# Two of the three split products of a 256-token segment taken as one 512-column stream

## The chip, the core and the metric

The kernel runs on one core of one Trainium2 chip. The metric is device microseconds of one execution. Before the change the median of three runs is 1772.79 us, from 1772.46 to 1773.16 us. The profile comes from one further execution, which took 1773.86 us, with 1771.5 us from its first to its last instruction. Its mean granted TensorE clock is 0.989 of full speed.

## The reference, cut to what matters

Two layers work on 768 tokens: 512 latent tokens and 256 context tokens, each 1024 wide. A layer mixes the tokens (four attention-like groups), projects the result back with the output weights, adds it to the stream, and then applies a gated feed-forward network (FFN) with a width-3 convolution over tokens. The second layer returns only the latent tokens.

```python
D_MODEL, SEQ, CTX_LEN, D_FF, DEPTH = 1024, 512, 256, 2816, 2

def dwconv3(x, w):
    xp = jnp.pad(x, ((0, 0), (1, 1), (0, 0)))
    return xp[:, :-2] * w[0] + xp[:, 1:-1] * w[1] + xp[:, 2:] * w[2]

# per layer, latent and context alike:
#   x = x + gate1 * (heads @ w_out)                      output projection
#   h = modulate(rmsnorm(x), shift, scale)
#   up = dwconv3(h @ w_up, w_conv) + b;  g, v = split(up)  up projection, 2 x 2816 wide
#   x = x + gate2 * ((silu(g) * v) @ w_down)             down projection
```

(The last four lines give the reference's loop body in short; the first part is word for word, apart from the constants being on one line.)

## The kernel before

Activations stand transposed: channels on the 128 partitions, tokens along the free dimension, so the 1024 channels are 8 tiles (`KT`). Each fp32 matrix product is made of three fp32r products: a weight is split into a rounded part `wh` and a rest `wl` (line 474 on ScalarE, line 478 on VectorE or GpSimd), an activation into `yh` and `yl`, and `product` (line 488) issues for each k-tile wh·yh, wh·yl and wl·yh into one PSUM tile. `self.mm` (line 73) records every matmul, so that all matmuls carry that line.

**Segments.** In layer 0 the tokens run as a 512-token segment and a 256-token context segment (`SEGS`). In layer 1 only 512 tokens are left; the output projection and the last part of the down projection run them as two halves of 256 (`HALVES`), the rest as one segment of 512. So 256-column matmuls stand at five places: the output projection of layer 0 for context (8 output tiles x 8 k-tiles = 64 k-steps), the up projection of layer 0 for context (44 units x 8 = 352), the down projection of layer 0 for context (8 x 22 = 176), the output projection of layer 1 (2 halves x 64 = 128), and the last chunk of the down projection of layer 1 (2 x 8 x 7 = 112). Together 832 k-steps.

**Output projection** (`w_out`): for each output tile eight k-steps into a PSUM bank `po`, then `residual` (line 883, VectorE): x = x + gate · po. While it runs, `tick` weaves in steps of the norm of the segment that is already done (`yt`, `yh`, `yl`, lines 397 to 407), in the order in which the program issues them on VectorE.

**FFN** (`ffn`): it is done in three chunks of 8, 7 and 7 pairs (`CHUNKS`). A pair is a gate unit and a value unit. A unit (`up`) takes eight k-steps into a PSUM tile `pu` of 1024 columns, of which there are two: latent in columns 0 to 511, context in 512 to 767. Then ScalarE writes `up` from `pu` (line 910), and VectorE adds the two outer taps of the convolution, reading `pu` (lines 912 and 915, each once for latent and once for context). `pu` is free after the last of these. The gate unit gets silu on ScalarE (line 926); the value unit is multiplied on GpSimd (line 935), rounded on ScalarE (`g`, line 937) and its rest formed on GpSimd (line 938). After each value unit of layer 0 up to two jobs from `todo` run: each is a pair of scans (`junk`, line 305, VectorE) that makes modulation numbers for later. After a chunk the down projection of its pairs runs into banks `pd`, each followed by `residual`.

The order on each engine is that in which the Python code issues the work; every engine takes its instructions in that order.

Of the kernel before, what the change touches and what calls it, by code (L numbers as in the profile page):

```python
# [16 lines left out]
KT = 8  # L17
SEQ = 512
# [34 lines left out]
class Trunk:  # L53
# [34 lines left out]
    def build(self):  # L88
# [1 line left out]
        ctx = self.ctx  # L90
        self.const = ctx.enter_context(self.pool("const", 1))
        self.wp = ctx.enter_context(self.pool("wp", 1))
        self.s3 = ctx.enter_context(self.pool("s3", 16))
        self.os = ctx.enter_context(self.pool("os", 3))
        self.sm = ctx.enter_context(self.pool("sm", 1))
        self.ps = ctx.enter_context(self.pool("ps", 1, space=bass.MemoryType.PSUM))
# [73 lines left out]
        for l in range(DEPTH):  # L170
# [29 lines left out]
                    self.tick(1)  # L200
            first = [self.up_open(l, 0, gv, True) for gv in range(2)]
            a, b = segs[0]
            part = lambda u, k0, k1: lambda: self.product(u[1][:, a:b], u[0], y, a, b, range(k0, k1))
            self.woven(steps, part(first[0], 0, 4), part(first[0], 4, 8), part(first[1], 0, 8))
            a, b = segs[1]
            self.pin = ALL
# [36 lines left out]
        fes.close()  # L243

    def new_y(self):
        return [tuple(self.s3.tile([128, T], F32R, tag="s3", name=n) for n in ("yh", "yl")) for _ in range(KT)]

    def mixing_pools(self, es):
        mk = lambda n, b: es.enter_context(self.pool(n, b, reuse_waits="tile"))
# [139 lines left out]
    def norm_apply(self, x, y, sg, A, sh, r, ks):  # L389
        nc = self.nc  # L390
        a, b = sg
        n = b - a
        j = 0 if b <= SEQ else 1
        for k in ks:
            t = self.u.tile([128, T], F32, tag="u", name="yt")
            yh, yl = y[k]
            i = nc.vector.scalar_tensor_tensor(out=t[:, :n], in0=x[k][:, a:b], scalar=A[:, k, j:j + 1],
                                               in1=r[:, :n], op0=ALU.mult, op1=ALU.mult)
            if self.ticking:
                self.tc.keep_in_program_order(i)  # L400
            nc.scalar.activation(out=yh[:, a:b], in_=t[:, :n], func=AF.Identity, bias=sh[:, k, j:j + 1])
            if self.slow and k % 2:
                nc.gpsimd.tensor_tensor(out=t[:, :n], in0=t[:, :n],
                                        in1=sh[:, k, j:j + 1].broadcast_to([128, n]), op=ALU.add)
                nc.gpsimd.tensor_tensor(out=yl[:, a:b], in0=t[:, :n], in1=f32v(yh[:, a:b]), op=ALU.subtract)  # L405
            else:
                nc.vector.scalar_tensor_tensor(out=yl[:, a:b], in0=t[:, :n], scalar=sh[:, k, j:j + 1],  # L407
                                               in1=f32v(yh[:, a:b]), op0=ALU.add, op1=ALU.subtract)
# [79 lines left out]
    def product(self, ps, w, y, a, b, ks=None):  # L488
        wh, wl = w
        n = len(y)  # L490
        for k in ks or range(n):
            yh, yl = y[k]
            self.mm(ps, lhsT=wh[:, k, :], rhs=yh[:, a:b], start=(k == 0), stop=False)
            self.mm(ps, lhsT=wh[:, k, :], rhs=yl[:, a:b], start=False, stop=False)
            self.mm(ps, lhsT=wl[:, k, :], rhs=yh[:, a:b], start=False, stop=(k == n - 1))


    def early_start(self, l, fast=False):
# [369 lines left out]
    def load_o(self, NT):  # L868
        nc = self.nc
        s = []  # L870
        for k in range(KT):
            g = self.g.tile([128, 2, T], F32R, tag="g", name="og")
            if k in self.kept:
                o = self.kept[k]
                nc.scalar.copy(out=g[:, 0, :NT], in_=o[:, :NT])
                nc.vector.tensor_tensor(out=g[:, 1, :NT], in0=o[:, :NT], in1=f32v(g[:, 0, :NT]), op=ALU.subtract)
            else:
                nc.sync.dma_start(out=f32v(g[:, :, :NT]), in_=self.od[:, k, :, :NT])
            s.append((g[:, 0], g[:, 1]))
        return s  # L880

    def residual(self, p, x, gate, m, a, b):
        self.nc.vector.scalar_tensor_tensor(out=x[m][:, a:b], in0=p[:, :b - a],  # L883
                                            scalar=gate[:, m, (0 if b <= SEQ else 1):(1 if b <= SEQ else 2)],
                                            in1=x[m][:, a:b], op0=ALU.mult, op1=ALU.add)

    def w_out(self, l, s, x, sg):
        a, b = sg
        for m in range(KT):
            w = self.weights(("wout", l, m), b - a == 256, m % 3 == 2 and l == 0)  # L890
            p = self.bank("tp", "po")
            self.product(p[:, :b - a], w, s, a, b)
            self.residual(p, x, self.mod[l][:, 16:24], m, a, b)
            self.tick(2 if m < 3 else 1)
        self.tick(KT)
# [2 lines left out]
    def up_open(self, l, i, gv, fast=False):  # L898
        return self.weights(("wup", l, i, gv), fast), self.ps.tile([128, 1024], F32, tag="sc", bufs=2, name="pu")

    def up(self, l, i, gv, y, segs, NT, opened=None):
        nc = self.nc
        w, p = opened or self.up_open(l, i, gv)
        if not opened:
            for a, b in segs:
                self.product(p[:, a:b], w, y, a, b)
        c0 = O_CONV + 4 * (i + NF * gv)
        cw = self.par[l][:, c0:c0 + 4]
        u = self.u.tile([128, T], F32, tag="u", name="up")
# [9 lines left out]
    def ffn(self, l, x, y, segs, first, todo, after):  # L919
# [10 lines left out]
        for k0, k1 in CHUNKS:  # L930
            G = []
            for i in range(k0, k1):
# [3 lines left out]
                gt = self.g.tile([128, 2, T], F32R, tag="g", name="g")  # L936
                nc.scalar.copy(out=gt[:, 0, :NT], in_=uv[:, :NT])
                eng.tensor_tensor(out=gt[:, 1, :NT], in0=uv[:, :NT], in1=f32v(gt[:, 0, :NT]), op=ALU.subtract)  # L938
                G.append((gt[:, 0], gt[:, 1]))
                for _ in range(2):  # L940
                    if todo:
                        todo.pop(0)()
# [3 lines left out]
            for sweep in sweeps:  # L946
                for m in range(KT):
                    w = self.weights(("wdn", l, m, k0, k1), sweep[0][1] - sweep[0][0] == 256,
                                     k1 == NF and m % 3 == 2 and l == 1)
                    for a, b in sweep:  # L950
                        p = self.bank("tp", "pd")
                        self.product(p[:, :b - a], w, G, a, b)
# [446 lines left out]
```

## Time and profile before

| | before |
|---|---|
| median of three runs | 1772.79 us |
| the profiled execution | 1773.86 us |
| its span | 1771.5 us |
| PE busy | 1676.8 us (95%) |
| DVE busy | 997.5 us (56%) |
| ACT busy | 788.7 us (45%) |
| POOL busy | 892.3 us (50%) |

PE is TensorE's matmul side, DVE is VectorE, ACT is ScalarE, POOL is GpSimd. Busy time is a mean over stages: an engine at 56% overall can be the one that everything waits for in one stage. A matmul's duration in the trace covers its way through the array; the next one starts before it ends, so the cost of one in a stream is the distance from one start to the next.

### The profile page before, as it was taken

What the parts mean: (1) busy time and instruction counts of PE and PEld (TensorE: products, weight loads), DVE (VectorE), ACT (ScalarE), POOL (GpSimd) and SP (SyncE); (2) the same over time, 40 slices, a digit from 0 to 9 for tenths busy, and PEclk for the clock granted to TensorE, in tenths of its full rate; (3) what the DMA queues carried; (4) which work ended last, traced back from release to release, by engine and by line L of the source; (5) the groups of instructions that cost most, each with busy time, mean ns of one, the idle gap of its engine ahead of it and who ended that gap; (6) DMA issues with size and microseconds to landing.
All of it is one profiled execution on the core that took longest, in us unless ns stands there. A gap on an engine that the chain in (4) does not pass through costs nothing. (4 is left out here: it accounts for less than half of the span.)

```text
span 1771.5 us, 26688 instructions
## 1 busy us (share of the span) xinstructions
PE 1676.8 (95%) x10212; PEld 1444.5 (82%) x10212; DVE 997.5 (56%) x1739; ACT 788.7 (45%) x1355; POOL 892.3 (50%) x700
## 2 busy tenths in 40 slices
PE   6899999899999999999999988999999999999997
PEld 4678778798888888888888786887789888888887
DVE  3577768653677854844255476886765522122245
ACT  4276655553543321332133354775654543242343
POOL 1323124665665643654365665323775666565663
PEclk9999999899999999999999999999999999999999
DMA  8665535336433332334343545542447333333334
GB/s 332 180 204 195 155 108 185 93 113 238 150 101 128 110 119 95 129 114 118 106 131 119 176 146 170 155 124 85 143 120 238 111 96 95 96 96 96 105 104 135
DMA packets 78447, 244.16 MB, mean 138 GB/s; under 512 B 9072, under 2 KB 12656, under 8 KB 78192
## 3 DMA queue, kind: packets, MB, share of 16 engines
q1 hardware_dynamic: 78320, 242.46, 43.5%
q8 instruction: 81, 1.33, 0.3%
q14 instruction: 46, 0.38, 0.1%
HBM read 214.64 MB, written 27.79 MB: 137 GB/s over the span
## 5 line engine op out<-in xcount | busy, mean ns | idle before, releaser
L478 POOL TENSOR_TENSOR wl<-raw,wh 128x1024 fp32r<-128x1024 f32 (+3 forms) x228 | 501.2, 2200 | 630.5 <-ACT wh L474 606.7
L474 ACT CAST wh<-raw 128x1024 fp32r<-128x1024 f32 (+1 forms) x228 | 233.6, 1027 | 356.0 <-PE pd L73 185.6
L73 PE MATMUL pu<-yh,wh 128*128 128x512 f32 (+1 forms) x1072 | 377.9, 353 | 6.0 <-DVE up L915 5.8
L73 PE MATMUL pu<-yl,wh 128*128 128x512 f32 (+1 forms) x1072 | 377.2, 352 | 1.5 <-POOL yl L405 1.3
L73 PE MATMUL pu<-yh,wl 128*128 128x512 f32 (+1 forms) x1072 | 376.4, 351 | 0.0
L73 PE MATMUL pd<-g,wh 128*128 128x512 f32 (+1 forms) x1168 | 289.3, 339 | 5.7 <-DVE x L883 3.7
L912 DVE SCALAR_TENSOR_TENSOR up<-pu,par,up 128x511 f32<-128x511 f32 (+1 forms) x132 | 83.1, 657 | 292.7 <-ACT up L910 291.2
L73 PEld LDWEIGHTS pu<-yh,wh 128*128 128x128 f32 x1072 | 202.8, 189 | 35.3 <-issue 6.2
L73 PEld LDWEIGHTS pd<-g,wh 128*128 128x128 f32 x1168 | 201.7, 191 | 31.6 <-ACT wh L474 3.9
L73 PEld LDWEIGHTS pu<-yl,wh 128*128 128x128 f32 x1072 | 202.8, 189 | 29.4 <-POOL yl L405 1.9
L73 PEld LDWEIGHTS pu<-yh,wl 128*128 128x128 f32 x1072 | 202.6, 189 | 27.1
L73 PE MATMUL pj<-yh,wh 128*128 128x512 f32 (+1 forms) x608 | 216.9, 360 | 6.9 <-ACT ev L552 4.4
L73 PE MATMUL pj<-yl,wh 128*128 128x512 f32 (+1 forms) x608 | 213.1, 351 | 1.6 <-DVE yl L407 1.4
L73 PE MATMUL pj<-yh,wl 128*128 128x512 f32 (+1 forms) x608 | 212.6, 350 | 0.1
L73 PE MATMUL pd<-g,wl 128*128 128x512 f32 (+1 forms) x584 | 197.3, 339 | 4.1 <-DVE wl L478 3.5
L305 DVE SCALAR_TENSOR_TENSOR junk<-mrow,cbc 128x1024 f32<-128x1024 f32 x80 | 155.3, 1942 | 1.5 <-DMA mrow<-in_wmodt 0.6
L883 DVE SCALAR_TENSOR_TENSOR x<-pd,mod,x 128x512 f32<-128x512 f32 (+1 forms) x80 | 48.8, 614 | 173.2 <-PE pd L73 173.0
L73 PEld LDWEIGHTS pj<-yh,wh 128*128 128x128 f32 x608 | 116.6, 192 | 26.2 <-ACT ev L552 7.3
L73 PEld LDWEIGHTS pj<-yh,wl 128*128 128x128 f32 x608 | 117.0, 192 | 15.1 <-POOL wl L478 0.5
L647 POOL TENSOR_TENSOR p<-p,rec 128x512 f32<-128x512 f32 (+2 forms) x80 | 79.7, 998 | 97.5 <-DVE rec L643 87.0
L73 PEld LDWEIGHTS pj<-yl,wh 128*128 128x128 f32 x608 | 117.4, 193 | 13.0 <-DVE yl L407 2.7
L73 PEld LDWEIGHTS pd<-g,wl 128*128 128x128 f32 x584 | 111.4, 191 | 17.0 <-DVE wl L478 4.3
(174 smaller groups left out, 2729.7 us busy)
## 6 DMA issues: line engine op xcount, KB each, us to landing
raw<-in_wup SPq DMA_DIRECT2D x88, 512.0 KB, 3.5
mrow<-in_wmodt SPq DMA_DIRECT2D x56, 512.0 KB, 3.6
raw<-in_win SPq DMA_DIRECT2D x44, 512.0 KB, 3.7
raw<-in_wdn SPq DMA_DIRECT2D x48, 448.0 KB, 3.4
mraw<-in_wmod SPq DMA_DIRECT2D x40, 512.0 KB, 7.3
raw<-in_wout SPq DMA_DIRECT2D x32, 512.0 KB, 3.5
qk<-hl SPq DMA_DIRECT2D x16, 768.0 KB, 3.5
stk<-qk SPq DMA_DIRECT2D x32, 384.0 KB, 5.6
```

What stands on the lines that cost most here:

```text
L73: i = self.nc.tensor.matmul(out, **kw)
L305: self.tc.keep_in_program_order(nc.vector.scalar_tensor_tensor(out=junk, in0=raw, scalar=1.0, in1=self.cbc[:, i], op0=ALU.mult, op1=ALU.mu ...
L474: i = nc.scalar.copy(out=wh, in_=raw)
L478: eng.tensor_tensor(out=wl[:, a:b], in0=raw[:, a:b], in1=f32v(wh[:, a:b]), op=ALU.subtract)
L647: self.nc.gpsimd.tensor_tensor(out=p, in0=p, in1=r.broadcast_to(list(p.shape)), op=ALU.mult)
L883: self.nc.vector.scalar_tensor_tensor(out=x[m][:, a:b], in0=p[:, :b - a], scalar=gate[:, m, (0 if b <= SEQ else 1):(1 if b <= SEQ else 2)] ...
L912: nc.vector.scalar_tensor_tensor(out=u[:, a + 1:b], in0=p[:, a:b - 1], scalar=cw[:, 0:1], in1=u[:, a + 1:b], op0=ALU.mult, op1=ALU.add)
```

## The change

The two parts of an activation are now one tile `[128, 2, T]`, so that a 256-token segment of both parts can be read as one stream of 2 x 256 columns. `product2` issues, for each k-tile, one matmul of wh with both parts (512 columns, into 512 PSUM columns: wh·yh in the first half, wh·yl in the second) and one of wl with yh (256 columns, into the first half). The two halves are added later. In the projections that end in a residual, `residual` runs once for each half. In the up projection of layer 0, `joined` has ScalarE copy the second half to SBUF and VectorE add it to the first half in PSUM, before the unit goes on. All 832 k-steps of 256 columns named above change from three matmuls to two; the 512-token segments keep `product`. The residuals of 256-token segments become 128 instead of 64 (8 + 24 + 16 + 16 more), and 44 copies and 44 adds are new.

```diff
     def new_y(self):
-        return [tuple(self.s3.tile([128, T], F32R, tag="s3", name=n) for n in ("yh", "yl")) for _ in range(KT)]
+        ys = [self.s3.tile([128, 2, T], F32R, tag="s3", name="y") for _ in range(KT)]
+        return [(y[:, 0], y[:, 1], y) for y in ys]
...
+    def product2(self, ps, w, y, a, b, ks=None):
...
+        wh, wl = w
+        n = len(y)
+        c = b - a
+        for k in ks or range(n):
+            yh, _, yb = y[k]
+            both = lambda: self.mm(ps[:, :2 * c].rearrange("p (s t) -> p s t", s=2), lhsT=wh[:, k, :],
+                                   rhs=yb[:, :, a:b], start=(k == 0), stop=(k == n - 1))
+            low = lambda: self.mm(ps[:, :c], lhsT=wl[:, k, :], rhs=yh[:, a:b], start=False, stop=False)
+            for f in (low, both) if k == n - 1 else (both, low):
+                f()
+
+    def joined(self, ps, c):
+
+        nc = self.nc
+        t = self.sm.tile([128, 256], F32, tag="mev", bufs=1, name="half")
+        nc.scalar.copy(out=t[:, :c], in_=ps[:, c:2 * c])
+        nc.vector.tensor_tensor(out=ps[:, :c], in0=ps[:, :c], in1=t[:, :c], op=ALU.add)
...
     def residual(self, p, x, gate, m, a, b):
-        self.nc.vector.scalar_tensor_tensor(out=x[m][:, a:b], in0=p[:, :b - a],
-                                            scalar=gate[:, m, (0 if b <= SEQ else 1):(1 if b <= SEQ else 2)],
-                                            in1=x[m][:, a:b], op0=ALU.mult, op1=ALU.add)
+        n = b - a
+        for c in range(0, 512, n):
+            self.nc.vector.scalar_tensor_tensor(out=x[m][:, a:b], in0=p[:, c:c + n],
+                                                scalar=gate[:, m, (0 if b <= SEQ else 1):(1 if b <= SEQ else 2)],
+                                                in1=x[m][:, a:b], op0=ALU.mult, op1=ALU.add)
+
+    def gated(self, p, w, y, a, b):
+        if b - a == 256:
+            self.product2(p, w, y, a, b)
+        else:
+            self.product(p[:, :b - a], w, y, a, b)
...
+    def up_product(self, p, w, y, a, b, ks=None):
+        if a == SEQ:
+            self.product2(p[:, SEQ:], w, y, a, b, ks)
+        else:
+            self.product(p[:, a:b], w, y, a, b, ks)
+
     def up(self, l, i, gv, y, segs, NT, opened=None):
...
             for a, b in segs:
-                self.product(p[:, a:b], w, y, a, b)
+                self.up_product(p, w, y, a, b)
+        if NT == T:
+            self.joined(p[:, SEQ:], CTX)
```

What this does to the order on the engines, at three places. First VectorE in the first chunk of layer 0's FFN, one round of a pair: the scans (`junk`) that follow a value unit, then the outer taps of the next gate unit and those of its value unit. Before:

```order
L305 SCALAR_TENSOR_TENSOR junk,mod_77<-mrow,cbc 128x1024 x2
L310 TENSOR_SCALAR mod_77<-mod_77,par_74 128x2
L305 SCALAR_TENSOR_TENSOR junk,mod_77<-mrow,cbc 128x1024 x2
L310 TENSOR_SCALAR mod_77<-mod_77,par_74 128x2
L912 SCALAR_TENSOR_TENSOR up<-pu,par_74,up 128x511
L912 SCALAR_TENSOR_TENSOR up<-pu,par_74,up 128x255
L915 SCALAR_TENSOR_TENSOR up<-pu,par_74,up 128x511
L915 SCALAR_TENSOR_TENSOR up<-pu,par_74,up 128x255
L912 SCALAR_TENSOR_TENSOR up<-pu,par_74,up 128x511
```

After the change, the same round:

```order
L306 SCALAR_TENSOR_TENSOR junk,mod_77<-mrow,cbc 128x1024 x2
L311 TENSOR_SCALAR mod_77<-mod_77,par_74 128x2
L306 SCALAR_TENSOR_TENSOR junk,mod_77<-mrow,cbc 128x1024
L517 TENSOR_TENSOR pu<-pu,half 128x256
L306 SCALAR_TENSOR_TENSOR junk,mod_77<-mrow,cbc 128x1024
L311 TENSOR_SCALAR mod_77<-mod_77,par_74 128x2
L950 SCALAR_TENSOR_TENSOR up<-pu,par_74,up 128x511
L950 SCALAR_TENSOR_TENSOR up<-pu,par_74,up 128x255
L953 SCALAR_TENSOR_TENSOR up<-pu,par_74,up 128x511
L953 SCALAR_TENSOR_TENSOR up<-pu,par_74,up 128x255
L517 TENSOR_TENSOR pu<-pu,half 128x256
L950 SCALAR_TENSOR_TENSOR up<-pu,par_74,up 128x511
```

The gate unit's add stands between the third and the fourth scan, the value unit's add between the gate unit's taps and its own. Next ScalarE in the same round, from the silu of a gate unit to the work of the next gate unit. Before:

```order
L926 ACTIVATE up<-up 128x768
L474 CAST wh<-raw 128x1024
L910 ACTIVATE up<-pu,par_74 128x768
L937 CAST g<-up 128x768
L474 CAST wh<-raw 128x1024
L910 ACTIVATE up<-pu,par_74 128x768
```

After:

```order
L964 ACTIVATE up<-up 128x768
L516 COPY half<-pu 128x256
L475 CAST wh<-raw 128x1024
L948 ACTIVATE up<-pu,par_74 128x768
L975 CAST g<-up 128x768
L516 COPY half<-pu 128x256
L475 CAST wh<-raw 128x1024
L948 ACTIVATE up<-pu,par_74 128x768
```

The copy stands in front of the weight cast in both units. Last, VectorE in layer 0's output projection of the context segment, from the fourth residual on, with the norm of the latent segment woven in. Before:

```order
L883 SCALAR_TENSOR_TENSOR x<-po,mod_77,x 128x256
L397 SCALAR_TENSOR_TENSOR yt<-x,affn_81,rb 128x512 x5
L478 TENSOR_TENSOR wl<-raw,wh 128x640
L407 SCALAR_TENSOR_TENSOR yl<-yt,mod_77,yh 128x512
L883 SCALAR_TENSOR_TENSOR x<-po,mod_77,x 128x256
L397 SCALAR_TENSOR_TENSOR yt<-x,affn_81,rb 128x512
```

After:

```order
L907 SCALAR_TENSOR_TENSOR x<-po,mod_77,x 128x256 x2
L398 SCALAR_TENSOR_TENSOR yt<-x,affn_81,rb 128x512 x6
L479 TENSOR_TENSOR wl<-raw,wh 128x640
L408 SCALAR_TENSOR_TENSOR y<-yt,mod_77,y 128x512
L907 SCALAR_TENSOR_TENSOR x<-po,mod_77,x 128x256
L408 SCALAR_TENSOR_TENSOR y<-yt,mod_77,y 128x512
L479 TENSOR_TENSOR wl<-raw,wh 128x640
L408 SCALAR_TENSOR_TENSOR y<-yt,mod_77,y 128x512
L907 SCALAR_TENSOR_TENSOR x<-po,mod_77,x 128x256 x2
```

Each residual is now two instructions; those of the fifth output tile stand apart, the second behind `y` (the former `yl`), `wl` and `y` again.

## Rows read from the trace of the kernel before

**Rows 1.** The page: busy time of the engines, share of the span, instructions.
```profile
PE 1676.8 (95%) x10212; PEld 1444.5 (82%) x10212; DVE 997.5 (56%) x1739; ACT 788.7 (45%) x1355; POOL 892.3 (50%) x700
```

**Rows 2.** The chain that ended last: start us, length us, what.
```profile
1403.95 81.87 PE pu L73 x360
1485.82 43.52 PE pd L73 x192
```

**Rows 3.** Timeline, PE, one unit's step from 512 to 256 columns (start, duration us).
```profile
565.19 0.39 PE L73 MATMUL pu<-yh,wl 128*128 128x512 f32 x1
565.41 0.28 PE L73 MATMUL pu<-yh,wh 128*128 128x256 f32 x1
...
568.16 0.28 PE L73 MATMUL pu<-yh,wl 128*128 128x256 f32 x1
```

**Rows 4.** Windows: us, busy us of each engine (instructions), clock, DMA share, GB/s.
```profile
455.00:481.00 26.00, 24.49 (x249) 23.28 (x248) 22.25 (x29) 16.61 (x25) 19.45 (x15) 1.00 0.40 125
...
500.00:640.00 140.00, 135.25 (x769) 118.64 (x770) 117.31 (x147) 42.93 (x50) 82.82 (x32) 1.00 0.37 122
640.00:706.00 66.00, 66.00 (x379) 58.32 (x380) 27.44 (x35) 8.30 (x8) 20.58 (x8) 1.00 0.28 92
...
757.00:980.00 223.00, 223.00 (x1282) 197.22 (x1281) 101.60 (x169) 62.86 (x68) 111.51 (x48) 1.00 0.40 118
980.00:1053.00 73.00, 67.31 (x414) 58.13 (x416) 43.43 (x64) 30.82 (x44) 44.23 (x28) 0.98 0.50 160
...
1342.00:1388.00 46.00, 44.31 (x412) 42.78 (x410) 32.27 (x46) 25.37 (x41) 32.23 (x28) 1.00 0.59 183
...
1714.00:1762.00 48.00, 45.23 (x410) 42.97 (x408) 27.76 (x45) 20.88 (x33) 20.14 (x19) 1.00 0.47 138
```

**Rows 5.** Waits of PE, 500 to 640 us: total us, times, longest us.
```profile
PE pu L73 <- DVE up L915: 4.5, 6, 1.4
```

**Rows 6.** Timeline, DVE, one round of a pair in the first chunk.
```profile
536.68 1.14 DVE L912 SCALAR_TENSOR_TENSOR up<-pu,par,up 128x511 f32<-128x511 f32 x2 [2.87 <-ACT up L910]
537.74 1.13 DVE L915 SCALAR_TENSOR_TENSOR up<-pu,par,up 128x511 f32<-128x511 f32 x2
538.78 1.22 DVE L305 SCALAR_TENSOR_TENSOR junk<-mrow,cbc 128x1024 f32<-128x1024 f32 x1
...
545.71 3.30 DVE L305 SCALAR_TENSOR_TENSOR junk<-mrow,cbc 128x1024 f32<-128x1024 f32 x1
...
549.19 1.13 DVE L912 SCALAR_TENSOR_TENSOR up<-pu,par,up 128x511 f32<-128x511 f32 x2
...
554.24 1.14 DVE L912 SCALAR_TENSOR_TENSOR up<-pu,par,up 128x511 f32<-128x511 f32 x2 [2.87 <-ACT up L910]
```

**Rows 7.** Timeline, ACT, the work within the second wait of 2.87 us.
```profile
551.46 0.84 ACT L926 ACTIVATE up<-up 128x768 f32<-128x768 f32 x1 [7.05 <-DVE up L915]
552.21 1.03 ACT L474 CAST wh<-raw 128x1024 fp32r<-128x1024 f32 x1
553.15 0.99 ACT L910 ACTIVATE up<-pu,par 128x768 f32<-128x768 f32 x1
```

**Rows 8.** Timeline, POOL, in the same round.
```profile
544.46 3.46 POOL L478 TENSOR_TENSOR wl<-raw,wh 128x1024 fp32r<-128x1024 f32 x1
```

**Rows 9.** Groups by line and shape: busy us, mean ns, idle before.
```profile
L283 ACT COPY mev<-macc 128x256 f32<-128x256 f32 x20 | 7.4, 370 | 15.3 <-PE macc L73 12.0 <-PE macc L77 3.3
L718 DVE TENSOR_TENSOR wtl<-wtp,wth 128x256 fp32r<-128x256 f32 x8 | 3.3, 416 | 0.1
L883 DVE SCALAR_TENSOR_TENSOR x<-pd,mod,x 128x256 f32<-128x256 f32 x40 | 19.0, 477 | 41.7 <-PE pd L73 41.6
```

**Rows 10.** Timeline, DVE, layer 0's output projection of the context segment.
```profile
468.64 0.47 DVE L883 SCALAR_TENSOR_TENSOR x<-po,mod,x 128x256 f32<-128x256 f32 x1
469.04 0.73 DVE L397 SCALAR_TENSOR_TENSOR yt<-x,affn,rb 128x512 f32<-128x512 f32 x1
```

**Rows 11.** Timeline, DVE, the last residual.
```profile
1761.69 0.48 DVE L883 SCALAR_TENSOR_TENSOR x<-pd,mod,x 128x256 f32<-128x256 f32 x1 [2.46 <-PE pd L73]
```

More of the change, by code (lines that the diff above doesn't have):

```diff
@@ L92, in build @@
         self.wp = ctx.enter_context(self.pool("wp", 1))
-        self.s3 = ctx.enter_context(self.pool("s3", 16))
+        self.s3 = ctx.enter_context(self.pool("s3", KT))
         self.os = ctx.enter_context(self.pool("os", 3))
@@ L202, in build @@
             a, b = segs[0]
-            part = lambda u, k0, k1: lambda: self.product(u[1][:, a:b], u[0], y, a, b, range(k0, k1))
+            part = lambda u, k0, k1: lambda: self.up_product(u[1], u[0], y, a, b, range(k0, k1))
             self.woven(steps, part(first[0], 0, 4), part(first[0], 4, 8), part(first[1], 0, 8))
@@ L395, in norm_apply @@
             t = self.u.tile([128, T], F32, tag="u", name="yt")
-            yh, yl = y[k]
+            yh, yl, _ = y[k]
             i = nc.vector.scalar_tensor_tensor(out=t[:, :n], in0=x[k][:, a:b], scalar=A[:, k, j:j + 1],
@@ L491, in product @@
         for k in ks or range(n):
-            yh, yl = y[k]
+            yh, yl, _ = y[k]
             self.mm(ps, lhsT=wh[:, k, :], rhs=yh[:, a:b], start=(k == 0), stop=False)
@@ L878, in load_o @@
                 nc.sync.dma_start(out=f32v(g[:, :, :NT]), in_=self.od[:, k, :, :NT])
-            s.append((g[:, 0], g[:, 1]))
+            s.append((g[:, 0], g[:, 1], g))
         return s
     def residual(self, p, x, gate, m, a, b):
-        self.nc.vector.scalar_tensor_tensor(out=x[m][:, a:b], in0=p[:, :b - a],
-                                            scalar=gate[:, m, (0 if b <= SEQ else 1):(1 if b <= SEQ else 2)],
-                                            in1=x[m][:, a:b], op0=ALU.mult, op1=ALU.add)
+        n = b - a
[8 more added lines that the diff above has]
+            self.product(p[:, :b - a], w, y, a, b)
     def w_out(self, l, s, x, sg):
@@ L891, in w_out @@
             p = self.bank("tp", "po")
-            self.product(p[:, :b - a], w, s, a, b)
+            self.gated(p, w, s, a, b)
             self.residual(p, x, self.mod[l][:, 16:24], m, a, b)
@@ L938, in ffn @@
                 eng.tensor_tensor(out=gt[:, 1, :NT], in0=uv[:, :NT], in1=f32v(gt[:, 0, :NT]), op=ALU.subtract)
-                G.append((gt[:, 0], gt[:, 1]))
+                G.append((gt[:, 0], gt[:, 1], gt))
                 for _ in range(2):
@@ L951, in ffn @@
                         p = self.bank("tp", "pd")
-                        self.product(p[:, :b - a], w, G, a, b)
+                        self.gated(p, w, G, a, b)
                         self.residual(p, x, gate, m, a, b)
```

## The prediction

> **What bounds the kernel now.** I read the page's table of busy times first: TensorE 95%, VectorE 56%, ScalarE 45% [rows 1]. That says that TensorE is the bound on average, so the next thing is to see where it is not, because the change takes work from TensorE and gives work to VectorE and ScalarE. The chain that ended last is almost only matmuls in its long pieces, without a gap: 360 of 512 columns in 81.87 us, so 227.4 ns each, and 192 in 43.52 us, 226.7 ns each [rows 2]. A 256-column matmul is read from the timeline: 23 distances between the starts at 565.41 and 568.16, 2.75 us, so 119.6 ns each; the step from a 512 to a 256 costs 0.22 us, no more than within the 512s [rows 3].
>
> Then the windows: in 640 to 706 us (down projection of the first chunk) and 757 to 980 us (units 22 to 43 of the up projection and the second chunk's down projection) TensorE is busy all of the time: 66.00 of 66.00 and 223.00 of 223.00 us. In five other windows that the change touches it is not: 455 to 481 (output projection, context) VectorE is busy 22.25 of 26 us; 500 to 640 (up projection of the first chunk) 117.31 of 140; and 980 to 1053, 1342 to 1388 and 1714 to 1762 show TensorE idle by 5.7, 1.7 and 2.8 us [rows 4]. The clock reads 1.00 in the windows in question (0.98 in one), the 2.4 GHz level, so it has no part in the sum.
>
> In 500 to 640 us TensorE waits 4.5 us in 6 waits for the taps that read `pu` [rows 5]. The round of a pair there repeats in 554.24 - 536.68 = 17.56 us: the value unit's taps, four scans, the next gate unit's taps at 549.19, then a wait of 2.87 us for ScalarE [rows 6]. In that wait ScalarE does silu, weight cast and `up`, one right behind the other: starts at 551.46, 552.21 and 553.15 [rows 7]. TensorE's work of a pair is 2 x 8 x 3 x (0.2274 + 0.1196) = 16.66 us, so the round is set by VectorE and ScalarE, and about 0.9 us of it is TensorE's slack. In that stretch nothing that TensorE saves counts.
>
> **The change part by part.** *TensorE.* A k-step of 256 columns takes 3 x 119.6 = 358.8 ns now, and 226.7 + 119.6 = 346.3 ns with the wide stream [rows 2, 3]: 12.5 ns less. Over 832 k-steps that is 10.4 us, if all of it counted. It counts in full where TensorE is busy all the time: 22 units x 8 = 176 k-steps, and 64 + 56 of the first two chunks' down projections, together 296, -3.7 us. In the first 22 units (176 k-steps), 16 in the first chunk and 6 in the second, I take it as nothing for the VectorE round, as long as two scans follow in each job: 24 jobs have two (8 for layer 0 and the first 16 for layer 1), 16 go to the first chunk's pairs, 4 to its down projection and 4 to two pairs of the second chunk; so there are 10 such rounds. The third pair of the second chunk I leave out of the gain too. The operand is read as two pieces of 256 with a stride; before has no such operand in these products. Between 0 and the whole 12.5 ns of a k-step, I take 0 as its cost.
>
> *A rule against this.* By the rows a matmul costs 119.6 ns for 256 columns and 226.7 for 512, so a fixed part of 2 x 119.6 - 226.7 = 12.5 ns is spared per matmul [rows 2, 3]. The Trainium skill (TensorE: Matmul & The Clock Gate, "Wait — 56ns, not 53.3ns?") says that the fixed part of a warm matmul is about 2.5 ns and that N columns otherwise take N / 2.4 GHz; by that the 296 k-steps would give back 0.7 us and not 3.7, and the sum below would be 3 us higher. The trace differs from it, and the measured distances decide.
>
> *ScalarE in the rounds.* The new copy of 128x256 from PSUM has a near row: 370 ns, and the ACT rows start about 0.09 us before the end of the one ahead (0.84 against 0.75, 1.03 against 0.94), so 0.28 us in line [rows 7, 9]. For the value unit it stands between silu and cast, right in the 2.87 us that VectorE waits. So each round gets 0.28 us longer: 10 x 0.28 = +2.8 us. For the gate unit it stands behind `g`, whose `up` is needed only after four scans; it is hidden by them.
>
> *VectorE in the rounds.* The add reads PSUM and SBUF, 128x256: the near row is 416 ns, 0.33 in line [rows 9]. The value unit's add falls into the 2.87 us of waiting, beside the cast, and delays `up` only if the copy is late; hidden. The gate unit's add stands between the third and the fourth scan. The fourth scan starts at 545.71 and takes 3.30 us where the first takes 1.22, and ends about 1.1 us after GpSimd's `wl` (544.46 + 3.46 = 547.92) [rows 6, 8]: it waits for GpSimd, not for VectorE. An add of 0.33 us ahead of it lies in that wait and costs nothing; if the cover is gone, it costs 0.33 in each of 10 rounds. The first pair of layer 0, which has nothing ahead of it to hide in, gets copy and add in line: +0.6. Copy and add in units 22 to 43 delay the release of `pu` by 0.6 us; TensorE is never idle there, and with 8.3 us per unit and two tiles I take them as hidden.
>
> *Residuals.* Each is one more instruction of 477 ns, 0.40 in line (468.64 to 469.04) [rows 9, 10]. In the down projections of the first two chunks VectorE has much idle time (27.44 of 66 busy) [rows 4]: nothing. Output projection of layer 0's context: 8 more, 3.2 us, and VectorE is at 22.25 of 26. From the fifth `yt` on it is without a gap; four to five more residuals there are 1.8 us, and the fifth tile's second one stands behind `y`, `wl` and `y` now, which I put at 0.5: +2.3; TensorE's 64 x 12.5 ns = 0.8 us is lost there. Bounds: -0.8 and +3.2. Third chunk of the down projection with the last pair ahead of it (980 to 1053): the last value unit's copy and add are partly in line, +0.4; 8 more residuals against 0.7 us of TensorE, +0.3. Layer 1's output projection: TensorE saves 128 x 12.5 = 1.6 us, VectorE gets 16 x 0.40 = 6.4 on 32.27 of 46 us; a third is left: -0.5, bounds -1.6 and +3.2 (half of the residuals fully in line). Layer 1's last chunk: 112 x 12.5 = 1.4 us against 6.4 us more on VectorE at 27.76 of 48; half of the gain is left, -0.7, some weights split on VectorE come later behind the residuals, +0.3, and the last residual is followed by nothing on TensorE but the norm [rows 11], so that one more is in line: +0.4. Sum 0, bounds -1.0 and +3.6.
>
> *The sum.* -3.7 + 2.8 + 0.6 + 2.3 + 0.7 - 0.5 + 0 = +2.2 us. Against the profiled execution that is 1773.86 + 2.2 = 1776.1; that execution lies 1.1 us above the median of the runs, so 1775.0 us on the median.
>
> **The rivals.** *Faster: the gain counts nearly everywhere.* If the waits in the VectorE rounds and the last windows only reflect when TensorE delivers, everything follows an earlier TensorE, and only the 10 copies and the last residual stay: -10.4 + 2.8 + 0.4 = -7.2, 1765.6 us. For it: TensorE is at 95% and its idle time in the layer 1 windows is small. Against: the round repeats to 0.02 us with TensorE idle in it [rows 5, 6].
>
> *Slower: the added VectorE work is in line.* Its place is the round and the windows of layer 1. If the add before the fourth scan isn't covered (GpSimd's `wl` starting later by the copy, and the scan with it), each of the 10 rounds gets 0.33 more, 3.3 us; and if half of layer 1's first 16 extra residuals delay the weight splits behind them, 8 x 0.40 = 3.2 us. Sum 2.2 + 6.5 = +8.7, 1781.5 us. It decides from the point where the fourth scan ends later than one copy's time after its place now. For it: VectorE is at 117.31 of 140 us there; against: the overlap with GpSimd above.
>
> *The wide stream spares nothing.* If the strided operand costs the 12.5 ns per k-step that it should spare, the 296 and the layer 1 gains go: +2.2 + 3.7 + 1.2 = +7.1, 1779.9 us. Against it: nothing in the rows speaks for such a cost.
>
> **How the numbers follow.** 0.45 for the forecast (its own range 1771 to 1779), 0.25 for the gain nearly everywhere (1762 to 1771), 0.22 for VectorE in line, 0.08 for a stream that spares nothing. A measurement can tell about 0.2%, 3.5 us, from no change: 1769.2 to 1776.3. Of the forecast's 0.45, 0.33 lie within it, 0.10 above and 0.02 below; of the faster rival 0.23 below and 0.02 within; of the last two, 0.03 within and 0.27 above. So 0.25 faster, 0.38 same, 0.37 slower. The range for 8 in 10: 1764 to 1783, from the faster rival with a bit of room to the slower one's price.
>
> **What would show it.** The round in the first chunk at 17.8 us, with silu, copy, cast and `up` in line in the wait, which then is about 3.15 us. The fourth scan ending where it ends now, relative to the round. TensorE at 346 ns per k-step in the context part of units 22 to 43, and 757 to 980 us about 2.9 us shorter. Layer 0's context output projection 2 us longer. The prediction is wrong if the round stays at 17.56 us or grows by over 0.5, if a k-step is not 346 ns, or if layer 1's two windows move by more than 1.5 us each.

## The result and the profile after

The changed kernel took 1784.67 us (median of six runs, 1782.85 to 1788.97), the kernel before 1772.62 us in the same sessions (1771.35 to 1773.43). The ratio is 1.0070, with an interval from 1.0059 to 1.0081: slower by 12 us. The forecast was 1775.0 us with a range of 1764 to 1783 us, so the time lies above the range. A slowdown of more than 0.2% had been given a chance of 0.37, no change beyond 0.2% one of 0.38.

The page's row of engines, to be read beside [rows 1]. Columns: busy time, share of the span, instructions.

```profile
PE 1673.3 (94%) x9380; PEld 1398.2 (78%) x9380; DVE 1038.2 (58%) x1847; ACT 803.3 (45%) x1399; POOL 893.3 (50%) x700
```

832 matmuls are gone, and TensorE's busy time fell by 3.5 us only; VectorE's rose by 40.7 us, ScalarE's by 14.6. VectorE has 108 instructions more, 64 residuals and 44 adds.

To see where the time went, I cut both timelines at instructions that both kernels have, and compare the lengths between them. The start times are those of the first or last residual of a group on VectorE (in the changed kernel the last second half) and of the `up` ACTIVATE of a unit on ScalarE, one profiled execution each; the end is the span on the page, to 0.1 us.

| stage | before, from - to | length | after, from - to | length | difference | forecast |
|---|---|---|---|---|---|---|
| first context residual of layer 0's output projection to the first `up` | 455.90 - 497.00 | 41.10 | 453.10 - 501.39 | 48.29 | +7.2 | +2.3 |
| first to 18th `up` (first chunk and its down projection) | 497.00 - 707.74 | 210.74 | 501.39 - 714.56 | 213.17 | +2.4 | +2.0 |
| 18th to 44th `up` | 707.74 - 984.36 | 276.62 | 714.56 - 989.73 | 275.17 | -1.4 | -2.3 |
| 44th `up` to the last context residual of the third chunk | 984.36 - 1052.89 | 68.53 | 989.73 - 1061.04 | 71.31 | +2.8 | +0.7 |
| first residual of layer 1's output projection to the 45th `up` | 1341.72 - 1401.46 | 59.74 | 1347.76 - 1410.32 | 62.56 | +2.8 | -0.5 |
| 88th `up` to the end | 1714.96 - 1771.50 | 56.54 | 1723.79 - 1782.60 | 58.81 | +2.3 | 0.0 |
| sum | | | | | +16.0 | +2.2 |

(The forecast of each stage is its terms in the prediction: 8 rounds at 0.28, the first pair's 0.6 and 0.8 for the down projection in the second line, 2 rounds, the 22 units' 2.2 and 0.7 in the third.) The span grew by 11.1 us, 4.9 less than the stages. The 4.9 lie where the change leaves the work as it was: 2.8 ahead of the first stage and 2.1 in layer 1's mixing, between the fourth stage and the fifth (286.72 us, before 288.83). Such starts move: the first residual of layer 0's output projection came anywhere from 413.33 to 421.26 us in the twelve profiled executions here, though no edit adds work ahead of it. So the experiments below are compared by these stages.

**The first stage.** TensorE's timeline in layer 0's output projection of the context, as in [rows 3].

```profile
467.85 0.40 PE L73 MATMUL po<-og,wh 128*128 128x512 f32 x1
475.11 0.76 PE L73 MATMUL po<-og,wh 128*128 128x512 f32 x1 [6.87 <-DVE x L907]
475.67 0.41 PE L73 MATMUL po<-og,wl 128*128 128x256 f32 x1
475.89 0.63 PE L73 MATMUL po<-og,wh 128*128 128x512 f32 x1
```

TensorE stands still for 6.87 us and waits for a residual. Two windows behind it, with the columns of [rows 4], show the granted clock, as a share of full speed:

```profile
477.00:479.00 2.00, 2.00 (x8) 1.71 (x7) 0.33 (x1) 0.78 (x2) 1.42 (x2) 0.50 0.00 0
...
481.00:483.00 2.00, 2.00 (x11) 1.76 (x12) 1.40 (x3) 1.28 (x3) 1.27 (x1) 1.00 0.00 0
```

The granted clock is 0.50 after the wait, the 1.2 GHz level, and 1.00 again from 481 us on. A k-step takes 0.64 us there (475.89 to 476.53), against 0.35 after; over the eight k-steps of one output tile that is 2.3 us more. What TensorE waited for is on VectorE's timeline, beside [rows 10]:

```profile
466.69 1.39 DVE L479 TENSOR_TENSOR wl<-raw,wh 128x640 fp32r<-128x640 f32 x1
468.00 1.48 DVE L408 SCALAR_TENSOR_TENSOR y<-yt,mod,y 128x512 fp32r<-128x512 f32 x1
469.41 0.47 DVE L907 SCALAR_TENSOR_TENSOR x<-po,mod,x 128x256 f32<-128x256 f32 x1
469.80 1.13 DVE L408 SCALAR_TENSOR_TENSOR y<-yt,mod,y 128x512 fp32r<-128x512 f32 x1
470.86 1.66 DVE L479 TENSOR_TENSOR wl<-raw,wh 128x640 fp32r<-128x640 f32 x1
472.43 1.74 DVE L408 SCALAR_TENSOR_TENSOR y<-yt,mod,y 128x512 fp32r<-128x512 f32 x1
474.10 0.86 DVE L907 SCALAR_TENSOR_TENSOR x<-po,mod,x 128x256 f32<-128x256 f32 x2
...
474.50 0.47 DVE L907 SCALAR_TENSOR_TENSOR x<-po,mod,x 128x256 f32<-128x256 f32 x1
```

(The row of 474.10 holds two instructions, `x2`; the last line is the second of them, from a narrower window.) The fifth output tile's first half is added at 469.41, its second half only at 474.50. Between the two stand `y`, `wl` and `y`, as the order shown ahead of the prediction says, and the first half of the sixth tile at 474.10. Until the second half is read, the bank is taken. `po` has two banks, so the seventh output tile cannot begin; TensorE goes on at 475.11, 0.14 us after that second half ends.

That order also shows an error in the description of the kernel before. It says that every engine takes its work in the order in which the code issues it. The code issues the two residuals side by side; what comes between them was put there by the planner that the kernel is built with, which may reorder the instructions of an engine, save those that the code pins.

**The same pattern** stands in the third chunk, on VectorE:

```profile
1047.19 0.47 DVE L907 SCALAR_TENSOR_TENSOR x<-pd,mod,x 128x256 f32<-128x256 f32 x1
1047.59 1.13 DVE L408 SCALAR_TENSOR_TENSOR y<-yt,mod,y 128x512 fp32r<-128x512 f32 x1
1048.64 1.66 DVE L479 TENSOR_TENSOR wl<-raw,wh 128x640 fp32r<-128x640 f32 x1
1050.22 1.75 DVE L408 SCALAR_TENSOR_TENSOR y<-yt,mod,y 128x512 fp32r<-128x512 f32 x1
1051.89 0.47 DVE L907 SCALAR_TENSOR_TENSOR x<-pd,mod,x 128x256 f32<-128x256 f32 x1
```

Here it is 4.7 us between the halves of the fifth tile. TensorE's waits for a residual (total, times, longest) grew in all four stages that have second residuals beside norm work. The first, fourth, fifth and sixth stage of the table, before (the fifth has no such wait):

```profile
PE po L73 <- DVE x L883: 0.7, 1, 0.7
PE pd L73 <- DVE x L883: 2.0, 2, 1.3
PE pd L73 <- DVE x L883: 0.3, 1, 0.3
```

and after:

```profile
PE po L73 <- DVE x L907: 6.9, 1, 6.9
PE pd L73 <- DVE x L907: 3.9, 2, 2.8
PE po L73 <- DVE x L907: 1.6, 1, 1.6
PE pd L73 <- DVE x L907: 1.4, 2, 1.2
```

The mean granted clock fell with them, from 1.00 to 0.89 in the first stage and from 0.98 to 0.93 in the fourth. The first stage, before and after, with the columns of [rows 4]:

```profile
455.90:497.00 41.10, 39.57 (x336) 35.90 (x335) 29.50 (x42) 24.19 (x38) 27.38 (x23) 1.00 0.44 154
```

```profile
453.10:501.39 48.29, 41.42 (x272) 34.30 (x271) 33.63 (x51) 25.07 (x38) 26.40 (x23) 0.89 0.37 131
```

**The rounds** of a pair came out as forecast. VectorE's timeline, one round, to be read beside [rows 6]:

```profile
542.34 1.14 DVE L950 SCALAR_TENSOR_TENSOR up<-pu,par,up 128x511 f32<-128x511 f32 x2 [1.48 <-ACT up L948]
...
551.24 0.42 DVE L517 TENSOR_TENSOR pu<-pu,half 128x256 f32<-128x256 f32 x1
551.57 3.07 DVE L306 SCALAR_TENSOR_TENSOR junk<-mrow,cbc 128x1024 f32<-128x1024 f32 x1
...
558.24 0.43 DVE L517 TENSOR_TENSOR pu<-pu,half 128x256 f32<-128x256 f32 x1 [1.23 <-ACT half L516]
560.15 1.14 DVE L950 SCALAR_TENSOR_TENSOR up<-pu,par,up 128x511 f32<-128x511 f32 x2 [1.48 <-ACT up L948]
```

The round takes 560.15 - 542.34 = 17.81 us, 0.25 more than the 17.56 of before. The fourth scan begins 0.33 us after the add does, which is 0.20 us later in the round than before (9.23 us after its start, before 9.03). It is shorter by 0.23 us, and ends 12.30 us after the round's start, where it ended 12.33 us after it before. In both kernels that end is 1.1 us behind the end of GpSimd's `wl` ([rows 6, 8] and this line of GpSimd's timeline: 550.11 + 3.45 = 553.56 against 551.57 + 3.07 = 554.64).

```profile
550.11 3.45 POOL L479 TENSOR_TENSOR wl<-raw,wh 128x1024 fp32r<-128x1024 f32 x1
```

The wait for ScalarE is filled on ScalarE as in [rows 7], with the copy in line:

```profile
557.10 0.85 ACT L964 ACTIVATE up<-up 128x768 f32<-128x768 f32 x1 [4.42 <-DVE up L953]
557.86 0.35 ACT L516 COPY half<-pu 128x256 f32<-128x256 f32 x1
558.11 1.05 ACT L475 CAST wh<-raw 128x1024 fp32r<-128x1024 f32 x1
559.06 0.99 ACT L948 ACTIVATE up<-pu,par 128x768 f32<-128x768 f32 x1
```

The copy takes 558.11 - 557.86 = 0.25 us of that line.

**The wide stream** on TensorE, in a unit where it never waits:

```profile
935.97 0.39 PE L73 MATMUL pu<-y,wh 128*128 128x512 f32 x1
936.19 0.28 PE L73 MATMUL pu<-y,wl 128*128 128x256 f32 x1
...
938.08 0.40 PE L73 MATMUL pu<-y,wh 128*128 128x512 f32 x1
```

Six k-steps take 938.08 - 935.97 = 2.11 us, 352 ns each, against 359 from [rows 3]. With 0.12 us for the 256-column matmul that leaves 0.23 us for the wide one, not 0.227. So 7 of the forecast 12.5 ns are spared. Over the 176 k-steps of the units in the third stage that is 1.0 us less gain; the stage fell 0.9 us short of its forecast.

### The profile page after: what moved, and what is told of

It is laid out like the page before. It is cut to its first block, busy times and chain, and to the rows that moved or that the text cites. A ratio compares the mean times of both kernels' runs of the same rounds, so it can differ in the third digit from the quotient of the medians.

```text
span 1782.6 us, 25148 instructions
## 1 busy us (share of the span) xinstructions
PE 1673.3 (94%) x9380; PEld 1398.2 (78%) x9380; DVE 1038.2 (58%) x1847; ACT 803.3 (45%) x1399; POOL 893.3 (50%) x700
## 5 line engine op out<-in xcount | busy, mean ns | idle before, releaser
L73 PE MATMUL pu<-y,wh 128*128 128x512 f32 (+1 forms) x1792 | 560.5, 388 | 12.0 <-DVE up L953 10.4
L73 PEld LDWEIGHTS pu<-y,wh 128*128 128x128 f32 x1792 | 331.5, 188 | 81.3 <-issue 10.8
L73 PE MATMUL pu<-y,wl 128*128 128x512 f32 (+1 forms) x1072 | 368.6, 351 | 0.0
L73 PE MATMUL pj<-y,wh 128*128 128x512 f32 (+1 forms) x1216 | 324.6, 354 | 7.7 <-ACT ev L574 4.9
L73 PE MATMUL pd<-g,wh 128*128 128x512 f32 x880 | 286.9, 396 | 7.8 <-DVE x L907 7.0
L73 PEld LDWEIGHTS pj<-y,wh 128*128 128x128 f32 x1216 | 206.7, 192 | 38.0 <-ACT ev L574 7.8
L73 PEld LDWEIGHTS pu<-y,wl 128*128 128x128 f32 x1072 | 201.6, 188 | 31.2
L73 PE MATMUL pj<-y,wl 128*128 128x512 f32 (+1 forms) x608 | 211.7, 349 | 0.1
L73 PEld LDWEIGHTS pj<-y,wl 128*128 128x128 f32 x608 | 116.5, 192 | 14.9 <-POOL wl L479 0.5
L73 PE MATMUL po<-og,wh 128*128 128x512 f32 x320 | 111.6, 406 | 9.0 <-DVE x L907 8.5
```

The lines of the kernel that those rows point to most:

```text
L73: i = self.nc.tensor.matmul(out, **kw)
```

## The experiments

All lengths are differences from the kernel before, in us, by the stages of the table above (S1 to S6 in its order), from one profiled execution of each kernel. The medians come from 2 to 12 runs.

| kernel | S1 | S2 | S3 | S4 | S5 | S6 | median | before, same sessions |
|---|---|---|---|---|---|---|---|---|
| changed kernel | +7.2 | +2.4 | -1.4 | +2.8 | +2.8 | +2.3 | 1784.67 | 1772.62 |
| tile_only | +3.1 | +0.1 | 0.0 | -1.3 | +0.7 | +0.1 | 1772.79 | 1772.40 |
| wout0_narrow | +3.2 | +3.6 | -1.5 | +2.1 | +1.4 | +3.3 | 1782.05 | 1772.40 |
| residual_once | +1.9 | +3.7 | -1.4 | -1.7 | +0.5 | -0.3 | 1773.59 | 1772.40 |
| four_banks | +4.3 | +2.5 | -1.4 | +2.8 | +1.3 | +2.4 | 1780.83 | 1772.40 |
| residual_twice | +6.4 | +0.1 | 0.0 | +5.3 | +2.1 | +4.5 | 1787.83 | 1773.63 |
| copy_add_alone | +3.9 | +20.8 | +7.0 | -2.2 | +0.7 | +1.7 | 1796.82 | 1773.63 |
| copy_first | +6.0 | +2.7 | -1.0 | +1.4 | +1.3 | +3.3 | 1781.78 | 1773.63 |
| busy_only | +2.9 | -0.4 | -1.6 | -1.7 | +0.7 | +0.9 | 1769.68 | 1773.63 |
| norm_later | +7.0 | +2.4 | -1.5 | +2.1 | +4.7 | +3.7 | 1786.94 | 1771.55 |
| busy_norm_later | +4.3 | -0.5 | -1.6 | -0.1 | +4.2 | -0.5 | 1775.99 | 1771.55 |

The runs of one kernel scatter more in these sessions than in the first one (before: 1766.72 to 1779.21 over 31 runs), so medians of few runs say less than the stages. S2 and S3 repeat to 0.1 us in the two kernels whose rounds are as before (tile_only and residual_twice).

**tile_only: the paired tile alone.**

```diff
-        if b - a == 256:
+        if False:
             self.product2(p, w, y, a, b)
...
-        for c in range(0, 512, n):
+        for c in (0,):
...
-        if a == SEQ:
+        if False:
             self.product2(p[:, SEQ:], w, y, a, b, ks)
...
-        if NT == T:
+        if False:
             self.joined(p[:, SEQ:], CTX)
```

> This kernel keeps the paired activation tile alone: every product is three matmuls again, one residual, no copy and add. Theory A (the loss comes from the second residuals and the copies, above all from one PSUM bank in layer 0's output projection that is given back late): no loss is left, and the 2.8 us by which the first output projection starts earlier stays, so 1769 to 1772 us. Rival B (the paired tile or another order of the instructions loses time by itself): above 1776 us.

The ratio to before is 1.0000 (0.9985 to 1.0016), 1772.79 us: a little above theory A's figure, far below rival B's. But S1 is 3.1 us longer already. TensorE's waits in 450 to 478 us:

```profile
PE po L73 <- ACT sq L338: 2.5, 1, 2.5
PE po L73 <- DVE x L907: 0.7, 1, 0.7
```

The wait for `sq` is 2.5 us, where before has 0.9 us in its stretch. The planner has put two `y` ahead of the sixth output tile's residual where before had one. So 3.1 of the 7.2 us come with the paired tile alone, without the stream or the sums; the median, within its interval, does not show them. Why the paired tile made the planner choose this order was not tried.

**wout0_narrow: layer 0's output projection as before, the rest changed.**

```diff
-            self.gated(p, w, s, a, b)
-            self.residual(p, x, self.mod[l][:, 16:24], m, a, b)
+            wide = l > 0
+            self.gated(p, w, s, a, b, wide)
+            self.residual(p, x, self.mod[l][:, 16:24], m, a, b, wide)
```

> The changed kernel, but with three matmuls and one residual in layer 0's output projection of the context tokens. Theory A (a bank held by the fifth output tile's second residual costs a wait of 6.9 us and a slow clock behind it): the stage from the first output projection to the first up unit goes from 82 back to about 75 us, so 7 us faster than the changed kernel, 1777 to 1778.5 us. Rival C (the stage is late because VectorE has more work, and what is taken from it here is lost again in the rounds behind): 1781 us or more.

S1 is +3.2, the same as with the paired tile alone; 4.0 us came back, not 7. S2 and S6 are 1.2 and 1.0 us longer than in the changed kernel, and the median, 1782.05 us, is within rival C's figure, not theory A's. So theory A is right on the place and too high on the size, and part of what S1 gave back was lost again behind it, as rival C has it.

**residual_once: every second residual left out.**

```diff
-        for c in range(0, 512, n):
+        for c in (0,):
```

> The changed kernel without the second residual in all 64 places (the second half of the PSUM columns is left out of the sum). Theory A: the fifth tile's bank in layer 0's output projection comes free 4 to 5 us earlier, and with it 5 to 6 us of the 7 go; layer 1's output projection gets 2 to 3 us and its last chunk 1 to 2 us back: 1773 to 1776 us. Rival C (the wide stream itself, not the residual, is what delays these stages): 1781 us or more.

1773.59 us, ratio 1.0005 (0.9989 to 1.0021). Against the changed kernel S1 is shorter by 5.3, S4 by 4.4, S5 by 2.3 and S6 by 2.5 us: 14.5 us in the four stages that have second residuals beside norm work. That is nearly all of the 15.1 us that these four stages grew by. Theory A holds; rival C, in the form that this run has it (the wide stream itself delays these stages), does not.

**four_banks: two more PSUM tiles for layer 0's context output tiles.**

```diff
             p = self.bank("tp", "po")
+            if a == SEQ and m in (4, 5):
+                p = self.ps.tile([128, 1024], F32, tag="sc", bufs=2, name="po")
```

> The changed kernel, with the fifth and sixth output tile of layer 0's context in the two PSUM tiles that are idle there, so that the seventh and eighth don't wait for the bank of the fifth. The second residual stays where it is or near it. Theory A: the wait of 6.9 us and the slow clock behind it are gone; VectorE's own work is still there, so 4 to 6 us faster than the changed kernel, 1779 to 1781 us. Rival C (VectorE's time sets this stage, whichever bank): within 1.5 us of the changed kernel, 1783 to 1786 us.

TensorE no longer waits for a residual in this stretch, 453 to 482 us; what it waits for is the squares of the context norm:

```profile
PE ms L73 <- ACT sq L338: 3.2, 3, 1.9
```

The median, 1780.83 us, lies within theory A's figure, but S1 is shorter by 2.9 us only than in the changed kernel, where theory A had 4 to 6. So the held bank with its slow clock is worth 2.9 us of the 7.2 and not the whole: behind the bank the next limit is the squares of the context norm, which ScalarE makes from what the residuals on VectorE leave.

**residual_twice: second residuals without the wide stream.**

```diff
-        for c in range(0, 512, n):
+        for c in ((0, 0) if n == 256 else (0,)):
```

(with the products of tile_only, and without copies and adds)

> The paired tile with three matmuls everywhere, and each 256-column residual issued twice on the same PSUM columns (so the product is added twice): the second residual without the wide stream. Theory A2 (the second residual itself delays banks and norm work, whatever TensorE does): against the paired tile alone the context part of layer 0's output projection gets 3 to 6 us longer, the third chunk's context down projection 3 to 4 us, layer 1's output projection 1.5 to 2.5 us and the end after layer 1's last up unit 2 to 3 us; in all 10 to 14 us. Rival D (these costs come only because TensorE delivers earlier and then waits): each below 1 us, in all below 4 us.

Against tile_only: S1 +3.3, S4 +6.6, S5 +1.3, S6 +4.3, in all 15.5 us, with 64 more instructions on VectorE and TensorE's work as before. That is more than theory A2's 10 to 14 us; S4 and S6 are above its figures, S5 a little below. Two of its stretches, 445 to 482 us and 1020 to 1066 us, show TensorE's waits for a residual:

```profile
PE po L73 <- DVE x L907: 5.5, 1, 5.5
...
PE pd L73 <- DVE x L907: 7.6, 1, 7.6
```

Rival D is out: the waits are there with an unchanged TensorE. It is the second residual and its place in VectorE's order.

**copy_add_alone: copies and adds without the wide stream.**

```diff
-        nc.scalar.copy(out=t[:, :c], in_=ps[:, c:2 * c])
+        nc.scalar.copy(out=t[:, :c], in_=ps[:, :c])
```

(with the products of tile_only, and one residual)

> The paired tile with three matmuls everywhere and one residual, but with the copy and add of each layer 0 unit (they add the unit's own columns, so the result is doubled there). Theory A: the round of a pair in the first chunk takes 17.8 us as in the changed kernel, so 2.5 to 3.5 us from the first to the 18th unit; nothing from unit 18 to 44. Rival E (the rounds got longer through the earlier TensorE or the late start): below 1 us.

A miss. The planner put the same instructions elsewhere: on VectorE the gate unit's add came behind the fourth scan, and on ScalarE the copies came behind the weight casts. VectorE's timeline:

```profile
540.91 1.14 DVE L950 SCALAR_TENSOR_TENSOR up<-pu,par,up 128x511 f32<-128x511 f32 x2 [1.13 <-ACT up L948]
...
553.14 0.42 DVE L517 TENSOR_TENSOR pu<-pu,half 128x256 f32<-128x256 f32 x1
...
554.70 1.14 DVE L950 SCALAR_TENSOR_TENSOR up<-pu,par,up 128x511 f32<-128x511 f32 x2 [1.01 <-ACT up L948]
...
560.63 1.14 DVE L950 SCALAR_TENSOR_TENSOR up<-pu,par,up 128x511 f32<-128x511 f32 x2 [1.13 <-ACT up L948]
```

The gate unit's `up` now waits for the add, and its taps for `up`. The round takes 560.63 - 540.91 = 19.72 us. It does not tell theory A from rival E; it shows what two copies and two adds cost per round in another place: 2.2 us instead of 0.25.

**copy_first: the value unit's copy ahead of the silu.**

```diff
-            nc.scalar.activation(out=ug[:, :NT], in_=ug[:, :NT], func=AF.Silu)
             return ug
...
-                uv = self.up(l, i, 1, y, cseg, NT, None if i else first[1])
+                silu = lambda: self.tc.keep_in_program_order(
+                    nc.scalar.activation(out=ug[:, :NT], in_=ug[:, :NT], func=AF.Silu))
+                uv = self.up(l, i, 1, y, cseg, NT, None if i else first[1], silu)
...
         if NT == T:
             self.joined(p[:, SEQ:], CTX)
+        if silu:
+            silu()
```

> The changed kernel with the value unit's copy ahead of the gate unit's silu on ScalarE, where it needs only TensorE, which is done with the unit by then. Theory A (0.28 us of a copy in line in each of ten rounds): the round is 17.5 to 17.6 us again, so first to 18th unit 2 to 2.8 us shorter than in the changed kernel. Rival E (the add or the wait for TensorE holds the round): 17.8 us as it is.

ScalarE's and then VectorE's timeline:

```profile
558.91 0.37 ACT L516 COPY half<-pu 128x256 f32<-128x256 f32 x1 [3.79 <-PE pu L73]
559.40 0.85 ACT L973 ACTIVATE up<-up 128x768 f32<-128x768 f32 x1
560.15 1.03 ACT L475 CAST wh<-raw 128x1024 fp32r<-128x1024 f32 x1
```

```profile
544.76 1.14 DVE L952 SCALAR_TENSOR_TENSOR up<-pu,par,up 128x511 f32<-128x511 f32 x2 [2.53 <-ACT up L950]
...
562.18 1.14 DVE L952 SCALAR_TENSOR_TENSOR up<-pu,par,up 128x511 f32<-128x511 f32 x2 [2.43 <-ACT up L950]
```

The round is 562.18 - 544.76 = 17.42 us, so the copy in line is what made it 17.81; rival E is out. But S2 did not get shorter, so the total that was expected of theory A did not come. Most of the loss lies in the first round: the second value unit's `up` comes 21.29 us after the first one's, against 19.24 in the changed kernel.

**busy_only: the wide stream only where TensorE is busy all the time.**

```diff
+                self.up_product(p, w, y, a, b, wide=i > 10)
+        if NT == T and i > 10:
             self.joined(p[:, SEQ:], CTX)
...
-                        self.gated(p, w, G, a, b)
-                        self.residual(p, x, gate, m, a, b)
+                        self.gated(p, w, G, a, b, k1 < NF)
+                        self.residual(p, x, gate, m, a, b, k1 < NF)
```

(and the output projections with three matmuls and one residual)

> The wide stream only where TensorE is busy all the time: units of pair 12 on in layer 0 (22 units), and the context part of the down projection of the first two chunks; everything else with three matmuls and one residual. Theory A: stage for stage as the paired tile alone, but 0.6 to 0.9 us less in the first chunk's down projection and 1.3 to 2.3 us less from unit 18 to 44: 1768.5 to 1772 us, 2 to 3 us below the paired tile alone. Rival B (another order loses what is gained): within 1 us of the paired tile alone or above.

1769.68 us over 12 runs against 1773.63, ratio 0.9975 (0.9963 to 0.9988): faster than both kernels. S2 and S3 together are 2.1 us shorter than with the paired tile alone, close to theory A. Against the kernel before, though, the six stages together are 0.8 us longer, so they do not show where the median's 4 us come from. In the profiled execution 3.6 us lie in layer 1's mixing, from the third chunk's last context residual to layer 1's first residual (285.23 us, before 288.83), whose code the edit leaves as it was. Whether that is the planner's order or chance is not shown; only the 2.1 us are traced to the wide stream.

**norm_later and busy_norm_later: one norm step instead of two behind the first three output tiles,** in the changed kernel and in busy_only.

```diff
-            self.tick(2 if m < 3 else 1)
+            self.tick(1)
```

> The changed kernel, with one norm step instead of two woven in behind each of the first three output tiles of an output projection: the same instructions, but on VectorE three of the latent segment's yt and not six stand ahead of the fifth tile's residuals in layer 0, and y and wl, not y, wl and y, between the two. Theory A3 (the place of the second residual in VectorE's order, not its time, keeps the bank): TensorE's wait of 6.9 us falls to 3 us or less and the context part of the output projection from 31.0 to 25 to 28 us, of which up to 2 us may come back before the first up unit because the norm ends later. Rival C2 (VectorE's load in this stretch sets its length, whatever the order): from the first context residual to the first up unit still 47.5 to 49 us.

> The wide stream only where TensorE is busy all the time, with one norm step instead of two behind the first three output tiles. Theory A3: layer 0's output projection loses the 3.2 us that it is longer than before, at most 1 us of it comes back before the first up unit; all else as with the wide stream in the busy stretches alone: 2 us below that, 1766 to 1769 us. Rival (the norm's end sets the stage): no gain, 1769 us or more.

In norm_later the bank came free earlier, and the time came back elsewhere. TensorE's timeline:

```profile
475.99 0.47 PE L73 MATMUL po<-og,wh 128*128 128x512 f32 x1 [2.51 <-DVE x L907]
...
484.77 1.05 PE L73 MATMUL ms<-sq,ones 128*32 128x64 f32 x24 [2.97 <-ACT sq L338]
487.05 1.36 PE L73 MATMUL ms<-sq,ones 128*32 128x64 f32 x32 [1.23 <-ACT sq L338]
```

The wait fell from 6.87 to 2.51 us, and from the first context residual to the first half of the last output tile it is 23.7 us instead of 31.0. But the norm ended later, and S1 is 48.1 us, +7.0, within rival C2's figures: all of the gain came back behind it. In busy_norm_later the same edit cost 1.4 us in S1 and 3.5 in S5, and the median is 1775.99 us, within its rival's figure too. Norm work taken out of TensorE's shadow is paid behind it. The edit moves two things, the residuals' place and the norm's end, so it does not measure what a better order alone would give.

## Why the prediction was wrong, step by step

**The step that failed is the cost of the second residuals.** They were priced at 0.40 us of VectorE time each, at +2.3 us with an upper bound of 3.2 in layer 0's output projection, and mostly hidden elsewhere, so that the four stages with residuals beside norm work came to +2.5 us. They measured +15.1. The residuals' own time was right: 0.47 us each, 0.40 in line. Leaving the second residuals out brought 14.5 us back in the four stages (residual_once), and adding them alone cost 15.5 us (residual_twice). There are 48 of them in these stages, 19.2 us at 0.40, so that three quarters or more of their time came out in the length, although VectorE has idle time there [rows 4].

What was missing is what waits for them. A residual frees a PSUM bank, and the squares of the next norm are made behind it. The order rows showed the fifth tile's halves with three instructions between them, and the prediction put 0.5 us on that; in the trace it is 5.1 us from half to half, a wait of 6.87 us on TensorE and 2.3 us of slower k-steps. The bank is not all of it: two more PSUM tiles brought back 2.9 of the 7.2 us in the first stage, and norm_later, which cut the wait to 2.51 us, brought back nothing; in both TensorE then waits for the norm's squares. How the cost divides between bank and norm in the other three stages was not tried.

**Missing: the planner.** S1 is 3.1 us longer with the paired tile alone. The prediction priced the new instructions, and no other move in the order that was shown. What made the planner choose another order stays open.

**TensorE's saving was too high.** The wide k-step was to be 346 ns and is 352 in the up projection; so the term for the strided operand, taken as 0 between bounds of 0 and 12.5 ns, is 5 to 6 ns there. In busy_only the 296 k-steps gave 2.1 us, not 3.7. The Trainium skill's figure, about 2.5 ns for the fixed part of a warm matmul (TensorE: Matmul & The Clock Gate, "Wait — 56ns, not 53.3ns?"), would have given an estimated 0.7 us (296 x 2.5 ns); the measured gain lies between the two.

**Its own signs.** Two of the prediction's signs of being wrong came: the k-step is not 346 ns, and both of layer 1's stages moved by more than 1.5 us.

**Right:** the rounds (17.81 us, forecast 17.8; S2 came out at +2.4 for +2.0), with the copy in line as their cause, shown by copy_first; the add before the fourth scan, hidden in the scan's wait for GpSimd; and the windows in which TensorE never waits as the place of a gain, shown by busy_only.

**The rivals.** The slower one had the right sign, and its price of 1781.5 us was 3 us short. Its place in the rounds was wrong: the fourth scan did not end later. Its place in the residuals was right, but hardly through the weight splits: TensorE's wait for those is 2.0 us in layer 1's output projection, where the paired tile alone has 1.8, and 0.8 us in the last stage as before. That the gain would count nearly everywhere is out, and so is a stream that spares nothing, since 7 of the 12.5 ns are spared.

## What to carry to other kernels

An instruction that reads a PSUM bank last also decides when TensorE may go on: price a second reader by the time from the first read to the last in the engine's order, look in that order for what stands between them, and then for what the next norm or product waits for once the bank is free. Put a change that buys TensorE time with work on another engine only where TensorE never waits. And cut the traces into stages at instructions that both kernels have, since a start that wanders by several us hides what a change of a few us does.

## What the runs showed of the hardware

After a wait of 6.87 us TensorE's granted clock was 0.50, the 1.2 GHz level, through some 5 us of full work (475 to 480 us), and a k-step took 0.64 us instead of 0.35. In norm_later, after a wait of 2.51 us, it was 1.00, the 2.4 GHz level (476 to 478 us), and a k-step took 0.35 us. A k-step with a 512-column operand read as two strided pieces of 256 took 352 ns in the up projection, 5 to 6 ns more than the 346 that a contiguous 512 and a 256 add up to; no run separates the stride from the change between 512 and 256 columns. The scan that waits for GpSimd got shorter by most of what was put ahead of it: 3.07 us for 3.30, behind an add of 0.33 in line, and its end stayed 1.1 us behind that of GpSimd's `wl`.
